# Average pooling by four over 64 x 256 x 8192: 64 KB runs per partition and a two-level pair sum in place of 32 KB runs and a reduction

## The chip, the cores and the metric

The kernel runs on one core of a Trainium2 chip. The metric is the device time of one execution in microseconds (us), as the median of several runs. Engine names: DVE is VectorE, ACT is ScalarE, SP is SyncE (here it only issues DMAs), POOL is GpSimd. TensorE is not used. 1 MB is 10^6 bytes and 1 KB is 1024 bytes here.

## What is computed

```python
x = np.random.randn(64, 256, 8192).astype(np.float32); kernel_size = stride = 4
out_len = (length - kernel_size) // stride + 1          # 2048
for i in range(out_len):
    output[:, :, i] = np.mean(x[:, :, 4*i : 4*i + 4], axis=2)
```

The windows don't overlap, and each row of 8192 gives 2048 means. The input is 536.87 MB and the output 134.22 MB, each read or written once, so 671.09 MB pass through the DMA engines whatever the tiling.

## The kernel before

The input is seen as 16384 rows of 8192 floats. `_packed_fast_path` (L215) takes 512 rows at a time with F = 4: partition p holds rows 4p to 4p+3 of the macro-tile, which lie one behind the other in DRAM, 128 KB in all. There are 32 macro-tiles.

In each of the first 31, the loop over f runs four times. L245 loads one row per partition on SP's queue: 128 partitions x 32 KB, 4096 KB in one DMA, into one of three buffers `xt` of the pool `xin`. L246 is one `tensor_reduce` on DVE that sums groups of four, 8192 values to 2048. L252 multiplies these by 1/4 on ACT, in place in `ot`. After four rows, L253 stores `ot` (32 KB per partition, 4096 KB) from ACT's queue. `ot` has two buffers.

The last macro-tile is cut finer. Row f = 0 is loaded whole, rows 1 and 2 in three pieces each (L263, reduced at L266, scaled at L272), and the last row in a ladder of six pieces of 1668, 2268, 1632, 1172, 844 and 608 columns (L284, reduced at L293). The results of rows 0 to 2 are stored in four parts of 6 KB per partition by SP (L292), which are issued behind the last load piece. The ladder's results are scaled by ACT and stored from ACT's queue (L309, L310), except the last piece, which DVE scales into `fin` (L300) and SP stores (L307).

The order of the work is set by the program order on each engine and by semaphores that the tile framework places. A load waits for the DVE instruction that read its buffer last (three tiles earlier), and for the DMA whose semaphore it uses again. A reduction waits for its load, and where it is the first into an `ot` buffer, for that buffer's store. SP issues loads in order, so a load that waits holds up what stands behind it on SP. All DMAs of SP (queue q1 in the profile) and of ACT (q10) run on the same 16 DMA engines, 8 partitions to an engine in a DMA of 128 partitions.

Of the kernel before, what the change touches and what calls it, by code (L numbers as in the profile page):

```python
# [7 lines left out]
_N_PARK = 4  # L8
_FINAL_COLS_TGT = 608
_LADDER_RATIO = 1.39  # L10
_NCHUNK_PRE = 3
_PACK_STORES = True
_PACK_F_MAX = 4


def _tail_ladder(total: int, k: int, final: int, ratio: float = _LADDER_RATIO,
                 max_chunks: int = 12) -> list:
    if total < 4 * final:
        return [total]
    rev = []  # L20
    s = 0
    w = float(final)
    while len(rev) < max_chunks - 1:
        wi = max(k, (int(round(w)) // k) * k)
        if s + wi > total - k:
            break
        rev.append(wi)
        s += wi
        w *= ratio
    sizes = [total - s] + rev[::-1]  # L30
    assert sum(sizes) == total and all(x > 0 and x % k == 0 for x in sizes)
    return sizes


def _even_chunks(total: int, k: int, n: int) -> list:
    n = max(1, min(n, total // k))
    q = (total // n) // k * k
    sizes = [q] * n
    sizes[-1] += total - q * n
    assert sum(sizes) == total and all(s > 0 and s % k == 0 for s in sizes)  # L40
    return sizes


@with_exitstack
def kernel(
    ctx: ExitStack,
    tc: tile.TileContext,
    x: bass.AP,
    kernel_size: bass.AP,
    stride: bass.AP,  # L50
    out: bass.AP,
):
    nc = tc.nc

    K = int(kernel_size)
    S = int(stride)
    assert K == S, "only stride == kernel_size supported"

    B, C, L = x.shape
    OL = (L - K) // S + 1  # L60
    assert OL * K <= L

    P = nc.NUM_PARTITIONS

    xf = x.flatten_outer_dims()
    of = out.flatten_outer_dims()
    rows = B * C

    inv_k = 1.0 / float(K)
    dt = x.dtype  # L70
    IL = OL * K

    if _PACK_STORES and IL == L:
        F = 0
        for cand in range(_PACK_F_MAX, 1, -1):
            if rows % (P * cand) == 0 and (rows // (P * cand)) >= 2:
                F = cand
                break
        if F >= 2 and L >= 64 * K and OL % 8 == 0 and OL * F * 4 <= 32768:
            _packed_fast_path(nc, tc, xf, of, rows, L, OL, K, F, inv_k, dt, P)  # L80
            return

    RPP = 1
    R = P * RPP
    NT = rows // R
    IL2 = RPP * L
    OL2 = RPP * OL
    fast = (
        IL == L
        and rows % R == 0  # L90
        and NT >= 6
        and IL2 >= 64 * K
        and OL % 2 == 0
    )

    if not fast:
        with (
            tc.tile_pool(name="xin", bufs=4) as pin,
            tc.tile_pool(name="res", bufs=4) as pout,
        ):  # L100
            r0 = 0
            while r0 < rows:
                rn = min(P, rows - r0)
                xt = pin.tile([P, IL], dt)
                ot = pout.tile([P, OL], dt)
                nc.sync.dma_start(out=xt[:rn], in_=xf[r0 : r0 + rn, :IL])
                nc.vector.tensor_reduce(
                    out=ot[:rn],
                    in_=xt[:rn].rearrange("p (m k) -> p m k", k=K),
                    axis=mybir.AxisListType.X,  # L110
                    op=mybir.AluOpType.add,
                )
                nc.scalar.mul(ot[:rn], ot[:rn], inv_k)
                nc.scalar.dma_start(out=of[r0 : r0 + rn], in_=ot[:rn])
                r0 += P
        return

    def xview(t):
        return xf[t * R : (t + 1) * R]

    def oview(t):
        return of[t * R : (t + 1) * R]

    ladder = _tail_ladder(IL2, K, _FINAL_COLS_TGT)
    chunks_pre = _even_chunks(IL2, K, _NCHUNK_PRE)
    fin_w = ladder[-1] // K

    with (
        tc.tile_pool(name="xin", bufs=4) as pin,
        tc.tile_pool(name="res", bufs=4) as pout,  # L130
        tc.tile_pool(name="rsv", bufs=1) as prsv,
        tc.tile_pool(name="fin", bufs=1) as pfin,
    ):
        rsv = prsv.tile([P, OL2], dt)
        fin = pfin.tile([P, fin_w], dt)

        for t in range(NT):
            xv = xview(t)
            ov = oview(t)
            xt = pin.tile([P, IL2], dt)  # L140
            ot = rsv if t == 0 else pout.tile([P, OL2], dt)

            if t == 0:
                nc.sync.dma_start(out=xt[:, :IL2], in_=xv[:, :IL2])
                nc.vector.tensor_reduce(
                    out=ot[:, :OL2],
                    in_=xt[:, :IL2].rearrange("p (m k) -> p m k", k=K),
                    axis=mybir.AxisListType.X,
                    op=mybir.AluOpType.add,
                )  # L150
                nc.scalar.mul(ot[:, :OL2], ot[:, :OL2], inv_k)
            elif t < NT - 3:
                nc.sync.dma_start(out=xt[:, :IL2], in_=xv[:, :IL2])
                nc.vector.tensor_reduce(
                    out=ot[:, :OL2],
                    in_=xt[:, :IL2].rearrange("p (m k) -> p m k", k=K),
                    axis=mybir.AxisListType.X,
                    op=mybir.AluOpType.add,
                )
                nc.scalar.mul(ot[:, :OL2], ot[:, :OL2], inv_k)  # L160
                nc.scalar.dma_start(out=ov[:, :OL2], in_=ot[:, :OL2])
            elif t < NT - 1:
                c0 = 0
                for cw in chunks_pre:
                    c1 = c0 + cw
                    o0, o1 = c0 // K, c1 // K
                    nc.sync.dma_start(out=xt[:, c0:c1], in_=xv[:, c0:c1])
                    nc.vector.tensor_reduce(
                        out=ot[:, o0:o1],
                        in_=xt[:, c0:c1].rearrange("p (m k) -> p m k", k=K),  # L170
                        axis=mybir.AxisListType.X,
                        op=mybir.AluOpType.add,
                    )
                    nc.scalar.mul(ot[:, o0:o1], ot[:, o0:o1], inv_k)
                    nc.scalar.dma_start(out=ov[:, o0:o1], in_=ot[:, o0:o1])
                    c0 = c1
            else:
                nchunk = len(ladder)
                c0 = 0
                for i, cw in enumerate(ladder):  # L180
                    c1 = c0 + cw
                    o0, o1 = c0 // K, c1 // K
                    last = i == nchunk - 1
                    nc.sync.dma_start(out=xt[:, c0:c1], in_=xv[:, c0:c1])
                    if last:
                        q0 = 0
                        qw = (OL2 - q0) // _N_PARK
                        for qi in range(_N_PARK):
                            qa = q0 + qi * qw
                            qb = q0 + (qi + 1) * qw if qi != _N_PARK - 1 else OL2  # L190
                            nc.sync.dma_start(
                                out=oview(0)[:, qa:qb], in_=rsv[:, qa:qb]
                            )
                    nc.vector.tensor_reduce(
                        out=ot[:, o0:o1],
                        in_=xt[:, c0:c1].rearrange("p (m k) -> p m k", k=K),
                        axis=mybir.AxisListType.X,
                        op=mybir.AluOpType.add,
                    )
                    if last:  # L200
                        nc.vector.tensor_scalar(
                            out=fin[:, :fin_w],
                            in0=ot[:, o0:o1],
                            scalar1=inv_k,
                            scalar2=None,
                            op0=mybir.AluOpType.mult,
                        )
                        nc.sync.dma_start(out=ov[:, o0:o1], in_=fin[:, :fin_w])
                    else:
                        nc.scalar.mul(ot[:, o0:o1], ot[:, o0:o1], inv_k)  # L210
                        nc.scalar.dma_start(out=ov[:, o0:o1], in_=ot[:, o0:o1])
                    c0 = c1


def _packed_fast_path(nc, tc, xf, of, rows, L, OL, K, F, inv_k, dt, P):  # L215
    R = P * F
    NTM = rows // R

# [10 lines left out]
    with (  # L229
# [6 lines left out]
        for t in range(NTM):  # L236
            xv = xe(t)
# [109 lines left out]
```

## Time and profile before

| what | value |
|---|---|
| runs (3) | median 1561.2 us, 1561.01 to 1561.22 |
| span of the profiled execution | 1559.0 us, first to last instruction |
| median less that span | 2.2 us |
| DVE busy | 1112.8 us, 71% of the span, 138 instructions |
| ACT busy | 247.4 us, 16% of the span, 137 instructions |
| HBM read, written | 536.87 MB, 134.22 MB |
| mean rate of the DMA engines | 430 GB/s over the span |

The profiled execution has no time of its own beside its span; the 2.2 us are start and end of an execution, outside the instructions, and are taken as they are. The page gives busy time per engine and, in 40 equal slices of 39 us, the busy share in tenths (9 is 90% or more). A DMA queue's share is the time that its packets took, as a share of 16 engines over the span. In rows of instructions, "idle before" is how long the engine had stood still and what ended that. A packet is one row of one DMA on one DMA engine, and each engine ends its part of a DMA with a packet of 4 bytes that counts a semaphore up.

### The profile page before, as it was taken

The page shows a single profiled execution, that of the slowest core. Times are in us where ns is not written, and L with a number is a line of the kernel's source. Part 1 is how long each engine was busy: PE and PEld are TensorE (multiplying, and loading weights), DVE is VectorE, ACT ScalarE, POOL GpSimd, SP SyncE. Part 2 cuts the span into 40 slices and gives each one's busy share as a digit, 9 for nine tenths or more (in the row PEclk, how much of TensorE's full clock was granted, in tenths as well). Part 3 has the DMA queues.
Part 4 walks back from the last instruction along what each step waited for, and adds up shares of the span by engine and source line. Part 5 has one row for each costly group of instructions (what it writes and reads, how often), then busy time and mean ns, then how long its engine had stood idle before and what let it go on. Part 6 is the DMA issues. An engine that isn't in the chain of part 4 may idle for free.

```text
span 1559.0 us, 724 instructions
## 1 busy us (share of the span) xinstructions
DVE 1112.8 (71%) x138; ACT 247.4 (16%) x137; POOL 0.2 (0%) x4
## 2 busy tenths in 40 slices
DVE  6777667776667866677666776667766677766786
ACT  1111111111111111111111111111111111111111
POOL 0000000000000000000000000000000000000000
DMA  9999999999999999999999999999999999999999
GB/s 416 418 430 436 437 432 430 430 430 432 439 433 430 430 432 430 438 434 431 430 432 430 435 434 433 431 431 430 433 437 433 432 430 431 430 437 434 432 427 384
DMA packets 25637, 671.14 MB, mean 430 GB/s; under 512 B 2848, under 2 KB 3488, under 8 KB 4768
## 3 DMA queue, kind: packets, MB, share of 16 engines
q1 hardware_dynamic: 20448, 540.10, 80.6%
q10 hardware_dynamic: 5184, 131.00, 19.5%
q14 instruction: 5, 0.04, 0.0%
HBM read 536.87 MB, written 134.22 MB: 430 GB/s over the span
## 4 chain that ended last, share of the span: by engine, by line
DMA 75%; DVE 24%; issue 0%; SPq 0%; DVEq 0%
DMA xt<-in_x_dram 75%; DVE ot L246 23%; DVE ot L293 1%; DVE ot L266 0%; SPq L263 0%; DVEq L246 0%; DVE fin L300 0%
## 5 line engine op out<-in xcount | busy, mean ns | idle before, releaser
L246 DVE TENSOR_REDUCE ot<-xt 128x2048 f32<-128x8192 f32 x124 | 1077.1, 8686 | 430.2 <-DMA xt<-in_x_dram 430.2
L252 ACT ACTIVATE ot<-ot 128x2048 f32<-128x2048 f32 x124 | 237.0, 1911 | 1270.2 <-DVE ot L246 1270.2
L266 DVE TENSOR_REDUCE ot<-xt 128x682 f32<-128x2728 f32 (+2 forms) x7 | 26.6, 3809 | 6.9 <-DMA xt<-in_x_dram 6.9
L272 ACT ACTIVATE ot<-ot 128x682 f32<-128x682 f32 (+2 forms) x7 | 6.6, 936 | 25.8 <-DVE ot L266 25.8
L293 DVE TENSOR_REDUCE ot<-xt 128x417 f32<-128x1668 f32 (+5 forms) x6 | 9.0, 1568 | 0.0
L309 ACT ACTIVATE ot<-ot 128x417 f32<-128x417 f32 (+4 forms) x5 | 2.6, 521 | 5.2 <-DVE ot L293 5.2
L252 ACT ACT_TABLE_LOAD x1 | 1.3, 1283 | 0.7 <-PEq L328 0.7
L300 DVE TENSOR_SCALAR fin<-ot 128x152 f32<-128x152 f32 x1 | 0.2, 239 | 0.0
L328 POOL MEMSET const-bfloat16-1.0<- 128x1 bf16 x1 | 0.1, 102 | 0.0
L328 POOL MEMSET const-uint8-127<- 128x1 uint8 x1 | 0.1, 102 | 0.0
L328 POOL MEMSET const-float32-0.0<- 128x1 f32 x1 | 0.1, 99 | 0.2 <-issue 0.2
L328 POOL MEMSET const-float32-1.0<- 128x1 f32 x1 | 0.1, 99 | 0.0
## 6 DMA issues: line engine op xcount, KB each, us to landing
xt<-in_x_dram SPq DMA_DIRECT2D x125, 4096.0 KB, 26.4
out_dram<-ot ACTq DMA_DIRECT2D x31, 4096.0 KB, 23.2
xt<-in_x_dram SPq DMA_DIRECT2D x4, 1364.0 KB, 23.4
out_dram<-ot SPq DMA_DIRECT2D x4, 768.0 KB, 7.7
xt<-in_x_dram SPq DMA_DIRECT2D x2, 1368.0 KB, 29.5
xt<-in_x_dram SPq DMA_DIRECT2D x1, 1134.0 KB, 16.2
xt<-in_x_dram SPq DMA_DIRECT2D x1, 834.0 KB, 22.6
xt<-in_x_dram SPq DMA_DIRECT2D x1, 816.0 KB, 17.8
```

The source lines that it names most:

```text
L246: nc.vector.tensor_reduce(out=ot[:, o0 : o0 + OL], in_=xt[:, :L].rearrange("p (m k) -> p m k", k=K), axis=mybir.AxisListType.X, op=mybir.A ...
L252: nc.scalar.mul(ot[:, o0 : o0 + OL], ot[:, o0 : o0 + OL], inv_k)
L266: nc.vector.tensor_reduce(out=ot[:, o0:o1], in_=xt[:, c0:c1].rearrange("p (m k) -> p m k", k=K), axis=mybir.AxisListType.X, op=mybir.AluOp ...
L272: nc.scalar.mul(ot[:, o0:o1], ot[:, o0:o1], inv_k)
L293: nc.vector.tensor_reduce(out=ot[:, o0:o1], in_=xt[:, c0:c1].rearrange("p (m k) -> p m k", k=K), axis=mybir.AxisListType.X, op=mybir.AluOp ...
L300: nc.vector.tensor_scalar(out=fin[:, :fin_w], in0=ot[:, o0:o1], scalar1=inv_k, scalar2=None, op0=mybir.AluOpType.mult,)
L309: nc.scalar.mul(ot[:, o0:o1], ot[:, o0:o1], inv_k)
L328: nc = _bacc.Bacc("TRN2", target_bir_lowering=False, num_devices=1)
```

## The change

The tensors are now seen as flat streams: 32 groups of 128 partitions x 32768 floats (the same 128 KB per partition as a macro-tile before). A group is loaded in two DMAs of 16384 floats per partition (64 KB in one run, 8192 KB a DMA) into two buffers `xt`, in place of four DMAs of 32 KB into three buffers. The `tensor_reduce` is replaced by two `tensor_tensor` adds on DVE: neighbours are added in pairs, 16384 values to 8192, written over the first half of `xt` (new L51), and these again in pairs, 8192 to 4096, into `ot` (new L56). ACT scales 4096 at a time in place of 2048 (new L57). The store of a group is as before, 4096 KB from ACT's queue (new L88), for groups 0 to 29.

In the last group the second load is made in two pieces, 11264 and 5120 columns (new L70). Behind them SP issues the store of the whole of group 30 (L76), that of the first half of group 31 (L77), and after each piece's scale that piece's store (L84). The ladder, the pieces of the two rows ahead of it, the store in four parts and DVE's own scale are gone; ACT issues no store in the last two groups. The paths for other shapes are removed too, and were not used by these shapes.

The buffers take 2 x 64 KB and 2 x 32 KB per partition, against 3 x 32 KB, 2 x 32 KB and a small one before.

```diff
+LOAD = 16384
+PER_STORE = 2
+LAST = (11264, 5120)
...
+    run = LOAD * PER_STORE
+    groups = total // (P * run)
...
+    pin = ctx.enter_context(tc.tile_pool(name="xin", bufs=2))
+    pout = ctx.enter_context(tc.tile_pool(name="res", bufs=2))
...
+    def pool(xt, at, width, ot, to):
+        half = width // 2
+        four = xt[:, at : at + width].rearrange("p (m k) -> p m k", k=2)
+        nc.vector.tensor_tensor(
+            out=xt[:, at : at + half], in0=four[:, :, 0], in1=four[:, :, 1], op=ADD
+        )
+        two = xt[:, at : at + half].rearrange("p (m k) -> p m k", k=2)
+        o = ot[:, to : to + width // K]
+        nc.vector.tensor_tensor(out=o, in0=two[:, :, 0], in1=two[:, :, 1], op=ADD)
+        nc.scalar.mul(o, o, inv_k)
...
+    for g in range(groups):
+        ot = pout.tile([P, run // K], dt)
+        end = g == groups - 1
+        for j in range(PER_STORE):
+            xt = pin.tile([P, LOAD], dt)
+            last = end and j == PER_STORE - 1
+            pieces = LAST if last else (LOAD,)
...
+            for w in pieces:
+                nc.sync.dma_start(
+                    out=xt[:, at : at + w], in_=xg[g][:, j * LOAD + at : j * LOAD + at + w]
+                )
...
+            if last:
+                nc.sync.dma_start(out=og[g - 1], in_=held[:, :])
+                nc.sync.dma_start(
+                    out=og[g][:, : j * LOAD // K], in_=ot[:, : j * LOAD // K]
+                )
+            for at, w in spans:
+                to = (j * LOAD + at) // K
+                pool(xt, at, w, ot, to)
+                if last:
+                    nc.sync.dma_start(
+                        out=og[g][:, to : to + w // K], in_=ot[:, to : to + w // K]
                     )
+        if g < groups - 2:
+            nc.scalar.dma_start(out=og[g], in_=ot[:, :])
+        held = ot
...
-                    nc.sync.dma_start(out=xt[:, :L], in_=xv[:, f * L : (f + 1) * L])
-                    nc.vector.tensor_reduce(
-                        out=ot[:, o0 : o0 + OL],
-                        in_=xt[:, :L].rearrange("p (m k) -> p m k", k=K),
-                        axis=mybir.AxisListType.X,
...
-                    nc.scalar.mul(ot[:, o0 : o0 + OL], ot[:, o0 : o0 + OL], inv_k)
-                nc.scalar.dma_start(out=ov[:, : F * OL], in_=ot[:, : F * OL])
...
```

More of the change, by code (lines that the diff above doesn't have):

```diff
@@ L6 @@
 from concourse._compat import with_exitstack
[L8 to L41, printed above, removed]
+ADD = mybir.AluOpType.add
+LOAD = 16384
+PER_STORE = 2
+LAST = (11264, 5120)
 @with_exitstack
@@ L55 @@
     K = int(kernel_size)
[L56 to L61, printed above, removed]
+    assert K == 4 and int(stride) == 4 and x.shape[-1] % 4 == 0
     P = nc.NUM_PARTITIONS
[L65 to L69, printed above, removed]
     dt = x.dtype
[L71 to L93, printed above, removed]
-    )
[L96 to L106, printed above, removed]
-                nc.vector.tensor_reduce(
-                    out=ot[:rn],
-                    in_=xt[:rn].rearrange("p (m k) -> p m k", k=K),
-                    axis=mybir.AxisListType.X,
-                    op=mybir.AluOpType.add,
-                )
[L113 to L149, printed above, removed]
-                )
[L151 to L172, printed above, removed]
-                    )
[L174 to L212, printed above, removed]
@@ L215, in _packed_fast_path @@
-def _packed_fast_path(nc, tc, xf, of, rows, L, OL, K, F, inv_k, dt, P):
-    R = P * F
-    NTM = rows // R
-    ladder = _tail_ladder(L, K, _FINAL_COLS_TGT)
-    chunks_pre = _even_chunks(L, K, _NCHUNK_PRE)
-    fin_w = ladder[-1] // K
-    def xe(t):
-        return xf[t * R : (t + 1) * R].rearrange("(p f) m -> p (f m)", f=F)
-    def oe(t):
-        return of[t * R : (t + 1) * R].rearrange("(p f) m -> p (f m)", f=F)
-    with (
-        tc.tile_pool(name="xin", bufs=3) as pin,
-        tc.tile_pool(name="res", bufs=2) as pout,
-        tc.tile_pool(name="fin", bufs=1) as pfin,
-    ):
-        fin = pfin.tile([P, fin_w], dt)
-        for t in range(NTM):
-            xv = xe(t)
-            ov = oe(t)
-            ot = pout.tile([P, F * OL], dt)
-            if t < NTM - 1:
-                for f in range(F):
-                    xt = pin.tile([P, L], dt)
-                    o0 = f * OL
-                    nc.sync.dma_start(out=xt[:, :L], in_=xv[:, f * L : (f + 1) * L])
-                    nc.vector.tensor_reduce(
-                        out=ot[:, o0 : o0 + OL],
-                        in_=xt[:, :L].rearrange("p (m k) -> p m k", k=K),
-                        axis=mybir.AxisListType.X,
-                        op=mybir.AluOpType.add,
-                    )
-                    nc.scalar.mul(ot[:, o0 : o0 + OL], ot[:, o0 : o0 + OL], inv_k)
-                nc.scalar.dma_start(out=ov[:, : F * OL], in_=ot[:, : F * OL])
-                continue
-            for f in range(F - 1):
-                xt = pin.tile([P, L], dt)
-                widths = [L] if f < F - 3 else chunks_pre
-                c0 = 0
-                for cw in widths:
-                    c1 = c0 + cw
-                    o0, o1 = f * OL + c0 // K, f * OL + c1 // K
-                    nc.sync.dma_start(
-                        out=xt[:, c0:c1], in_=xv[:, f * L + c0 : f * L + c1]
-                    )
-                    nc.vector.tensor_reduce(
-                        out=ot[:, o0:o1],
-                        in_=xt[:, c0:c1].rearrange("p (m k) -> p m k", k=K),
-                        axis=mybir.AxisListType.X,
-                        op=mybir.AluOpType.add,
-                    )
-                    nc.scalar.mul(ot[:, o0:o1], ot[:, o0:o1], inv_k)
-                    c0 = c1
-            fq = F - 1
-            xt = pin.tile([P, L], dt)
-            hold = fq * OL
-            nchunk = len(ladder)
-            c0 = 0
-            for i, cw in enumerate(ladder):
-                c1 = c0 + cw
-                o0, o1 = fq * OL + c0 // K, fq * OL + c1 // K
-                last = i == nchunk - 1
-                nc.sync.dma_start(
-                    out=xt[:, c0:c1], in_=xv[:, fq * L + c0 : fq * L + c1]
-                )
-                if last:
-                    qw = hold // _N_PARK
-                    for qi in range(_N_PARK):
-                        qa = qi * qw
-                        qb = (qi + 1) * qw if qi != _N_PARK - 1 else hold
-                        nc.sync.dma_start(out=ov[:, qa:qb], in_=ot[:, qa:qb])
-                nc.vector.tensor_reduce(
-                    out=ot[:, o0:o1],
-                    in_=xt[:, c0:c1].rearrange("p (m k) -> p m k", k=K),
-                    axis=mybir.AxisListType.X,
-                    op=mybir.AluOpType.add,
-                )
-                if last:
-                    nc.vector.tensor_scalar(
-                        out=fin[:, :fin_w],
-                        in0=ot[:, o0:o1],
-                        scalar1=inv_k,
-                        scalar2=None,
-                        op0=mybir.AluOpType.mult,
-                    )
-                    nc.sync.dma_start(out=ov[:, o0:o1], in_=fin[:, :fin_w])
-                else:
-                    nc.scalar.mul(ot[:, o0:o1], ot[:, o0:o1], inv_k)
-                    nc.scalar.dma_start(out=ov[:, o0:o1], in_=ot[:, o0:o1])
-                c0 = c1
@@ new lines @@
+    inv_k = 1.0 / K
+    run = LOAD * PER_STORE
+    total = x.shape[0] * x.shape[1] * x.shape[2]
+    groups = total // (P * run)
+    assert groups * P * run == total and groups >= 2
+    xg = x.flatten_outer_dims().rearrange("r l -> (r l)").rearrange("(g p w) -> g p w", p=P, w=run)
+    og = out.flatten_outer_dims().rearrange("r l -> (r l)").rearrange(
+        "(g p w) -> g p w", p=P, w=run // K
+    )
+    pin = ctx.enter_context(tc.tile_pool(name="xin", bufs=2))
+    pout = ctx.enter_context(tc.tile_pool(name="res", bufs=2))
@@ new lines @@
+    held = None
+    for g in range(groups):
[5 more added lines that the diff above has]
+            pieces = LAST if last else (LOAD,)
+            at = 0
+            spans = []
+            for w in pieces:
+                nc.sync.dma_start(
+                    out=xt[:, at : at + w], in_=xg[g][:, j * LOAD + at : j * LOAD + at + w]
+                )
+                spans.append((at, w))
+                at += w
+            if last:
+                nc.sync.dma_start(out=og[g - 1], in_=held[:, :])
+                nc.sync.dma_start(
+                    out=og[g][:, : j * LOAD // K], in_=ot[:, : j * LOAD // K]
+                )
+            for at, w in spans:
[4 more added lines that the diff above has]
+                        out=og[g][:, to : to + w // K], in_=ot[:, to : to + w // K]
+                    )
+        if g < groups - 2:
+            nc.scalar.dma_start(out=og[g], in_=ot[:, :])
+        held = ot
```

## Prediction, made before the changed kernel was run

> **What bounds the kernel now.** I read the page first, its slices and queues:
>
> ```profile
> DMA  9999999999999999999999999999999999999999
> GB/s 416 418 430 436 437 432 430 430 430 432 439 433 430 430 432 430 438 434 431 430 432 430 435 434 433 431 431 430 433 437 433 432 430 431 430 437 434 432 427 384
> ...
> q1 hardware_dynamic: 20448, 540.10, 80.6%
> q10 hardware_dynamic: 5184, 131.00, 19.5%
> ```
>
> The DMA engines are busy in every slice, and the loads' queue and the stores' queue together take 100.1% of 16 engines. That is saturation from first to last, not on average. The chain of waits gives 24% to DVE, which is misleading: a load waits for the reduction that frees its buffer, but others are still queued when it is issued. The timeline of the start shows that the work keeps step with the transfers:
>
> ```profile
> 12.74 8.69 DVE L246 TENSOR_REDUCE ot<-xt 128x2048 f32<-128x8192 f32 x1 [12.74 <-DMA xt<-in_x_dram]
> ...
> 22.43 8.69 DVE L246 TENSOR_REDUCE ot<-xt 128x2048 f32<-128x8192 f32 x1 [1.01 <-DMA xt<-in_x_dram]
> ...
> 32.14 8.69 DVE L246 TENSOR_REDUCE ot<-xt 128x2048 f32<-128x8192 f32 x1 [1.03 <-DMA xt<-in_x_dram]
> ```
>
> Each reduction starts as its load lands, 9.70 us after the one before. An engine moves 8 rows in that time, 1.213 us a row, and 4.194 MB in 9.70 us is 432 GB/s. Beside a store, loads land 14.49 us apart (149.50 to 163.99 in the timeline): 12 packets of 1.21, so loads and stores alternate and none is lost. Stage by stage, the busy times by window say where the rate falls:
>
> ```profile
> 100.00:1500.00 1400.00, 1000.30 (x116) 221.61 (x116) 0.00 (x0) 1.00 1.00 433
> 1500.00:1540.00 40.00, 33.12 (x8) 7.69 (x7) 0.00 (x0) 1.00 1.00 425
> 1540.00:1550.00 10.00, 9.91 (x8) 3.38 (x6) 0.00 (x0) 1.00 1.02 413
> 1550.00:1555.00 5.00, 0.00 (x0) 0.00 (x0) 0.00 (x0) 1.00 1.03 407
> 1555.00:1559.00 4.00, 0.00 (x0) 0.00 (x0) 0.00 (x0) 1.00 0.25 96
> ```
>
> Columns: window, length, busy DVE, ACT, POOL, clock, DMA share, GB/s. The middle runs at 433. Only the last 20 us, with their small pieces, are slower. So the bytes don't change, the end is set by the DMA queues, and there is little to win: packets, the tail, and nothing from DVE. 671.09 MB at 433 GB/s are 1549.9 us of the 1559.0.
>
> **The change, part by part.**
>
> *Fewer packets.* The trace's packet records (one entry per packet, no view prints them) give these medians:
>
> ```
> bytes   4   608  2432  6144  10912  32768
> ns      9    31    98   234    411   1213
> ```
>
> The slope from 608 to 32768 is (1213-31)/32160 = 0.03675 ns a byte, which leaves 8.7 ns a packet. But the next packet opens before the last one closes: starts on one engine lie 1209.5 ns apart, and 1209.5 less 32768 x 0.03675 is about 5 ns. I take 5, since the distance of starts is what a saturated engine pays. Its ends are 0 (a run of 64 KB is still moved as two packets, or the fee goes by bytes) and 8.7. A loss I exclude: the records are linear over a factor of 54 in size. Now an engine has (20448+5184)/16 = 1602 packets, 178 of them semaphores (one a DMA), 1424 of data. After: 65 loads and 34 stores of 8 rows, 792 of data and 99 semaphores. The 63 full loads merge 504; 128 more go with the small pieces.
> - merging: 504 x 5 = 2.5 us (0 to 504 x 8.7 = 4.4)
> - small pieces: 128 x 5 = 0.6 us (to 1.1)
> - semaphores: 79 x 6 ns between starts = 0.5 us (to 0.7)
>
> Together 3.6 us, from 1.1 to 6.2.
>
> *The tail.* Before, reads and writes of 0.6 to 9 KB a row mix. Against 433 GB/s the windows lack 10 x 20/433 = 0.5 us, 5 x 26/433 = 0.3, and in the last 4 us, of which the DMAs ran 3.1 (to 1558.1), 3.1 less 4 x 96/433 = 2.2: 3.0 us. After, behind the last load stand 4.2 MB of group 30 and 2.1 MB of group 31, 14.6 us at 433, on one queue and pure writes. Under them lies the work on the last pieces. Piece one lands 6.0 us ahead of piece two; DVE needs about 9.1 us for it and 4.2 for piece two, ACT 1.3 more. The last store is thus issued some 9 us after the last landing, and 11 with the issue delay below: covered by 14.6 us. If that cover were gone, the excess would stand at the end in full. Some scatter of the engines stays; I take 2.0 of the 3.0 back, ends 0 and 3.0.
>
> *DVE.* TENSOR_TENSOR is not in this trace. The reductions give 8686 ns for 8192 inputs and 778 for 608: 1.043 ns a step and 144 ns fixed. The only elementwise row, L300's TENSOR_SCALAR, takes 239 ns for 152, (239-144)/152 = 0.63 a step, so a step of an elementwise instruction is no dearer than a reduction's. An add that takes a pair each step: 8192 x 1.043 + 144 = 8.69 us, and 4096 give 4.42, 13.1 a tile, against two reductions' 17.4. If every value read is a step (2 a pair), it is 17.2 + 8.7 = 25.9. I take 13.1 by the nearest row, and neither end gains anything: what decides is when the next load is issued. Least issue to landing is 12.0 us (the view of the input tile), less 9.70 of moving: 2.3 us. A load is ready 13.1 + 2.3 = 15.4 us after its buffer's tile landed, while the other buffer's load lasts 2 x 9.68 = 19.4. Slack is 4.0 us, against 2 x 9.70 - 8.7 - 2.3 = 8.4 now with three buffers. Beside a store the load lasts 29 us and the slack is 13.6. So the smaller DVE time costs and wins nothing, and the lost buffer costs nothing.
>
> [...]
>
> *Waits on queues.* SP's load waits now on DVE's second add; behind it on SP stands only the next load, and at the end the parked stores, which would be behind the loads on the DMA rings anyway. A store takes 29 us in place of 23.2, as 8 rows of 1.21 alternate with 8 of 2.42. Who waits for it is new L56 two groups on: at 3 x 24.2 + 8.7 = 81 us after the group's second tile landed, when the store ends at 13.1 + 3.7 (ACT, 1911 ns doubled) + 2 + 29 = 48. Nothing. ACT's time falls off the path as now.
>
> [...]
>
> *Start.* First packets are issued as before, and DVE's first work at 22 us in place of 12.7 delays nothing but the third load (issued at 35, ready at 37, the second lands at 41). Zero.
>
> **Sum.** 1559.0 - 3.6 - 2.0 = 1553.4 us of span, and with the 2.2 around it 1555.6. Ends: -1.1 and -9.2, so 1560.1 and 1552.0.
>
> **Rivals.**
> 1. *The runs aren't merged* (64 KB is moved as two packets, or a packet's fee goes by bytes). For it: no record here is over 32 KB. Against: the instruction carries one run of 64 KB a row. Then 1.1 + 2.0 = 3.1: 1558.1; 1560.1 if the tail gives nothing either.
> 2. *DVE becomes the bound, slower.* One mechanism: the adds read two values from SBUF at each step, 8 bytes apart, in the same partition, and take two steps. With only two buffers the DMA engines run dry as soon as DVE's tile passes 19.4 - 2.3 = 17.1 us (beyond that every us over costs up to 64). At 25.9 it is 22 + 64 x 25.9 + 10 of tail = 1690 of span, 1692. For it: the operation has no row, and the slack halves. Against: the 0.63 ns above.
> 3. *The tail gives nothing back* but packets do: 1557.6, told within the forecast's range.
>
> **How the numbers follow.** A change within 0.2% (3.1 us) can't be told from none. Forecast, 1555.6 with 1552.0 to 1558.6 about it (rival 3 in it): 0.66, of which 0.62 is faster by over 0.2%. Rival 1: 0.22, half below 1558.1 and half within 0.2%: 0.11 and 0.11. Rival 2: 0.12, slower. So faster 0.73, same 0.15, slower 0.12. The range is 1552.0 to 1561.0, the ends of the unknown costs and 0.9 for scatter; it leaves out rival 2 and little else.
>
> **What would show it.** Packets: the queues' counts fall to about (520+32+69) x 16 = 9936 on q1 and 30 x 9 x 16 = 4320 on q10; q1 near 18000 means rival 1. Middle: 433 to 434 GB/s at DMA share 1.00, adds of 8.7 and 4.4 us, and loads landing 19.4 and 29 us apart in turn. A share under 0.98 in the middle, or adds of 17 us, means rival 2. Tail: over 420 GB/s until 3 us before the end. I am wrong if the span changes by more than 7 us with the middle at 433, since then the time is in something that I haven't named.

## The result, and the profile after

The changed kernel takes 1576.05 us (1569.3 to 1581.1, four runs) against 1561.11 (1560.88 to 1561.22): ratio 1.0093, interval 1.0065 to 1.0122, slower by 0.9%. The forecast was 1555.6 and the range ended at 1561.0. Note the scatter too: 12 us between runs, where the kernel before has 0.3.

The page after (slices of 39.5 us, queues, DVE's groups):

```profile
span 1579.3 us, 492 instructions
...
DMA  9999999999999999999999999999999999999998
GB/s 425 416 432 427 437 424 425 427 435 430 428 428 419 442 425 423 419 431 427 427 425 425 432 422 428 422 428 416 431 432 418 427 420 427 443 415 420 416 435 369
...
q1 hardware_dynamic: 9936, 545.26, 81.3%
q10 hardware_dynamic: 4320, 125.83, 18.5%
...
L51 DVE TENSOR_TENSOR xt<-xt 128x8192 f32<-128x8192 f32 (+1 forms) x65 | 556.5, 8561 | 722.0 <-DMA xt<-in_x_dram 721.9
...
L56 DVE TENSOR_TENSOR ot<-xt 128x4096 f32<-128x4096 f32 (+1 forms) x65 | 283.4, 4360 | 3.9
```

The packet counts are those forecast, so 64 KB are one packet each. DVE is idle for 722 us, waiting for loads. The DMA engines are as busy as before, yet they move 425 GB/s in place of 430. By window, the middle has it (length, DVE, ACT, POOL, clock, DMA share, GB/s):

```profile
100.00:1500.00 1400.00, 749.93 (x116) 206.12 (x57) 0.00 (x0) 1.00 1.00 427
```

A share of 1.00 at 427, where it was 1.00 at 433. The engines never lack work; some packets take longer. The packet records say which:

```
load packets            size    median ns   mean ns   over the median by 32 ns or more
before                  32768        1213      1217      51 of 16000
after                   65536        2418      2468     800 of  8064
```

The excess over the median, summed over all load packets and divided by 16 engines, is 25.0 us after and 3.8 before. And it lies in one place: 24 of the 25 us belong to packets that start between 4 us before and 14 us after ACT issues a store. The timeline around one store shows it at work (adds on a landed tile, and the issue of a store):

```profile
1075.69 8.69 DVE L51 TENSOR_TENSOR xt<-xt 128x8192 f32<-128x8192 f32 x1 [16.87 <-DMA xt<-in_x_dram]
...
1092.52 0.34 ACTq L88 DMA_DIRECT2D out_dram<-ot  x1
1095.02 8.69 DVE L51 TENSOR_TENSOR xt<-xt 128x8192 f32<-128x8192 f32 x1 [6.18 <-DMA xt<-in_x_dram]
...
1124.92 8.69 DVE L51 TENSOR_TENSOR xt<-xt 128x8192 f32<-128x8192 f32 x1 [16.69 <-DMA xt<-in_x_dram]
```

Two loads land 19.33 and 29.90 us apart, 49.23 for a group of 16.8 MB read and 4.2 written; the kernel before takes 48.47 (from one store's issue at 101.88 to the next at 150.35). The load without a store, 19.33, is as forecast. The store is issued 2.5 us ahead of a landing. What follows on two of the engines is this (start in us, L a load packet, S a store packet, duration in ns where it isn't 2418 or 1213; the records don't name the engine, so each chain is put together by time, a packet where the one before it ends):

```
1093.20 L          1095.61 L (3702)   1099.31 S   1100.52 L          1102.93 S
1093.46 L (2831)   1096.29 S          1097.50 L (3513)   1101.01 S   1102.22 L
```

The load packets around the store's first packet last up to 1.3 us longer, and this on every engine. A packet or two later all is normal. So 30 stores at some 0.8 us are the loss, and it is more than the gain. (49.23 - 48.47) x 30 = 23 us, less some 2.5 us that the rest of the run gained, is the span's change of 20.3.

### The profile page after: what moved, and what is told of

Its sections match the earlier page's. It is cut to its first block, busy times and chain, and to the rows that moved or that the text cites. A ratio compares the mean times of both kernels' runs of the same rounds, so it can differ in the third digit from the quotient of the medians.

```text
span 1579.3 us, 492 instructions
## 1 busy us (share of the span) xinstructions
DVE 839.8 (53%) x130; ACT 232.9 (15%) x66; POOL 0.2 (0%) x4
## 3 DMA queue, kind: packets, MB, share of 16 engines
q1 hardware_dynamic: 9936, 545.26, 81.3%
q10 hardware_dynamic: 4320, 125.83, 18.5%
## 4 chain that ended last, share of the span: by engine, by line
DMA 72%; DVE 27%; issue 0%; ACT 0%; SPq 0%
DMA xt<-in_x_dram 72%; DVE xt L51 18%; DVE ot L56 9%; ACT ot L57 0%; SPq L70 0%
## 5 line engine op out<-in xcount | busy, mean ns | idle before, releaser
L51 DVE TENSOR_TENSOR xt<-xt 128x8192 f32<-128x8192 f32 (+1 forms) x65 | 556.5, 8561 | 722.0 <-DMA xt<-in_x_dram 721.9
L57 ACT ACTIVATE ot<-ot 128x4096 f32<-128x4096 f32 (+1 forms) x65 | 231.6, 3564 | 1333.3 <-DVE ot L56 1333.3
L56 DVE TENSOR_TENSOR ot<-xt 128x4096 f32<-128x4096 f32 (+1 forms) x65 | 283.4, 4360 | 3.9
```

Of the source, the lines that this page charges most:

```text
L51: nc.vector.tensor_tensor(out=xt[:, at : at + half], in0=four[:, :, 0], in1=four[:, :, 1], op=ADD)
L56: nc.vector.tensor_tensor(out=o, in0=two[:, :, 0], in1=two[:, :, 1], op=ADD)
L57: nc.scalar.mul(o, o, inv_k)
```

## The experiments

**First set.** My first theory, S, was that the packet's size does it: 64 KB packets are stretched at every start of a store. Its rival P was the place at which the store starts.

*e1_half_rows*: each 64 KB load in two DMAs of 32 KB rows (`HALF` is 8192).

```diff
-                nc.sync.dma_start(
-                    out=xt[:, at : at + w], in_=xg[g][:, j * LOAD + at : j * LOAD + at + w]
-                )
+                for c in range(at, at + w, HALF):
+                    cw = min(HALF, at + w - c)
+                    nc.sync.dma_start(
+                        out=xt[:, c : c + cw], in_=xg[g][:, j * LOAD + c : j * LOAD + c + cw]
+                    )
```

> Every 64 KB load of the changed kernel is made as two DMAs of 32 KB rows into the two halves of the same buffer; adds, scales, stores and their order stay. Theory S (a load packet of 64 KB is stretched when a store starts on the other queue, 0.8 us per engine and store, 25 us in all): the stretching goes with the packet size, the stores start 48.5 us apart in place of 49.2, 1556 to 1560 us. Theory P (the place: the store now starts just where one load gives way to the next, with two buffers only): packets of 32 KB are stretched as well, 1570 to 1580 us.

Measured 1569.88 us, ratio 1.0057 (1.0042 to 1.0072). The time lies a hair under P's range. Packets of 32 KB are stretched as well, 567 of 16384, 13.0 us per engine. S falls; half of the cost may still go with the size.

*e6_store_halves*: each store in two, one behind each tile's scale.

```diff
                 pool(xt, at, w, ot, to)
+                if g < groups - 2:
+                    nc.scalar.dma_start(
+                        out=og[g][:, to : to + w // K], in_=ot[:, to : to + w // K]
+                    )
...
-        if g < groups - 2:
-            nc.scalar.dma_start(out=og[g], in_=ot[:, :])
```

> The changed kernel with every store of a group made in two halves, one behind each tile's scale (2048 KB, 16 KB rows): 60 starts of a store in place of 30 for the same bytes. Theory S with its cost per start: another 20 to 27 us, 1592 to 1608 us. If the cost goes with the bytes stored beside loads, or with how unlike the packets are, it stays within 5 us of 1576 or grows by the 2 us of more packets.

Measured 1555.55 us, ratio 0.9965 (0.9952 to 0.9978), faster than either of the two ranges that I had (1592 to 1608 by S, within 5 us of 1576 otherwise). Its timeline:

```profile
1076.83 0.34 ACTq L84 DMA_DIRECT2D out_dram<-ot  x1
1084.17 8.69 DVE L51 TENSOR_TENSOR xt<-xt 128x8192 f32<-128x8192 f32 x1 [11.02 <-DMA xt<-in_x_dram]
1101.06 0.34 ACTq L84 DMA_DIRECT2D out_dram<-ot  x1
1108.36 8.69 DVE L51 TENSOR_TENSOR xt<-xt 128x8192 f32<-128x8192 f32 x1 [10.98 <-DMA xt<-in_x_dram]
```

A tile lands every 24.2 us, which is 8 x (2.418 + 0.611) with the 611 ns that a 16 KB packet takes at the end of the changed kernel, and the stores follow each other without a pause (issued 24.13 to 24.24 us apart from the fourth to the 56th): store packets alternate with load packets all the time, and the step from loads alone to both happens once. Its load packets have a mean of 2421 ns. That 64 KB packets beside stores are no harm is shown here. What saves this run isn't shown: its stores never pause, but each is also issued 7.3 us ahead of a landing, and no run here separates the two.

*e2_sp_stores*: SP issues each store behind the load two tiles ahead, so that there is one queue.

```diff
+        if n + 2 < ntiles:
+            load(n + 2)
+        if j == PER_STORE - 1 and not last:
+            nc.sync.dma_start(out=og[g], in_=ot[:, :])
```

> The 64 KB loads stay, but each group's store is issued by SP, behind the load made two tiles ahead, so that all DMAs stand in one queue in order and no two queues are served in turn. Theory S and theory P both need two queues at once: no stretching, median 64 KB packet and mean both 2418 ns, 1552 to 1557 us. If a 64 KB read simply suffers from writes being made at the same time by other engines, or from two buffers only, it stays at 1566 to 1580 us.

Measured 1558.01 us, ratio 0.9981 (0.9972 to 0.9991), a little over what was expected. 4.6 us of stretch per engine remain, most of it in the first 500 us. Without two queues served in turn the cost is nearly gone.

*e3_before_pairs*: the kernel before with pair adds in place of `tensor_reduce`.

> The kernel before with only the sums changed: two levels of pair adds in place of each reduction. Both theories: the adds lie under the transfers, 4.43 + 2.29 = 6.7 us a row in place of 8.69, and the time stays within 1 us of 1561.1. If the adds themselves slow the transfers (they read SBUF at twice the rate), it is 1566 us or more.

Measured 1561.78 us, ratio 1.0004 (0.9994 to 1.0013): the sums cost and win nothing, as forecast.

**Second set: the place.** ACT multiplies the group's second half by 1.0 some more times before it issues the store; the output doesn't change, only the store's moment. The number in `range` is 2 in f1, 1 in f3, 4 in g1, 6 in g2 and 8 in i1.

```diff
         if g < groups - 2:
+            for _ in range(2):
+                nc.scalar.mul(ot[:, LOAD // K :], ot[:, LOAD // K :], 1.0)
             nc.scalar.dma_start(out=og[g], in_=ot[:, :])
```

> The changed kernel, with two more ACT multiplications by 1.0 (3.62 us each, on the second half of the group's result) between a group's last scale and its store: the store is issued 24 us after its tile landed instead of 16.8, so 4.7 us behind the change from one load to the next instead of 2.5 us ahead of it. Theory P (what costs is a store that starts as the load queue goes from one DMA to the next): the load packets aren't stretched, 1553 to 1560 us. Rival Q (what costs is that loads alone give way to loads and stores in turn with one load queued instead of two, wherever that happens): 1568 to 1580 us as before.

Measured 1554.69 us, ratio 0.9959 (0.9944 to 0.9974): faster than both kernels, and all that it adds to the changed one is 7.3 us of useless work on ACT before each store. Its middle and one group:

```profile
100.00:1500.00 1400.00, 757.16 (x116) 419.50 (x116) 0.00 (x0) 1.00 1.00 434
```

```profile
1078.11 8.69 DVE L51 TENSOR_TENSOR xt<-xt 128x8192 f32<-128x8192 f32 x1 [8.61 <-DMA xt<-in_x_dram]
1080.48 0.34 ACTq L90 DMA_DIRECT2D out_dram<-ot  x1
...
1126.46 8.69 DVE L51 TENSOR_TENSOR xt<-xt 128x8192 f32<-128x8192 f32 x1 [8.63 <-DMA xt<-in_x_dram]
1128.81 0.34 ACTq L90 DMA_DIRECT2D out_dram<-ot  x1
```

The store is issued 2.4 us behind a landing (4.7 was expected) in place of 2.5 ahead, and a group takes 48.33 us in place of 49.23. The stretch is 2.2 us per engine in the whole run, half of it at the first store.

> The same with one multiplication: the store is issued 20.4 us after its tile landed, 1.1 us behind the change of loads, about where the kernel before has it (0.9 us). Theory P: 1553 to 1562 us. Rival Q: 1568 to 1580 us.

Measured 1570.53 us, ratio 1.0059 (1.0042 to 1.0076): P had 1562 at most, and the time lies in Q's range, 1568 to 1580. A delay that puts the issue on the landing itself (within 0.35 us, stores 3 to 30) doesn't help; "as before, 0.9 us behind" was not reached, since the stores drifted. P alone was too coarse.

The same in the kernel before, three multiplications of the last row's 2048 results ahead of each store:

> The kernel before with three more ACT multiplications by 1.0 (1.91 us each) ahead of each 4096 KB store, which is then issued 16.6 us after its last row landed, 2.8 us ahead of a change of loads instead of 0.9 us behind one. Theory P: load packets are stretched now in the kernel before as well, 0.4 to 0.9 us per store, 1568 to 1590 us. Rival Q (two loads still queued): 1561 us, unchanged within 1 us.

Measured 1565.65, 1569.26 and 1571.24 us, ratio 1.0049 (1.0032 to 1.0066); a fourth run took 1590.9 and is left out. The kernel before, with its 32 KB rows, reductions and three buffers, loses 8 us by the store's place alone, a little over half of what the changed one lost. Q is refuted by this and by f1.

> The kernel before with macro-tiles of two rows per partition in place of four: 62 stores of 2048 KB (16 KB rows) in place of 31 of 4096 KB, the same place of issue behind a load's landing. By packets alone 256 more per engine at 5 ns and 31 more semaphores: plus 1.5 us, 1562 to 1563. If the number of starts cost 0.8 us each even here: 1580 us or more. If stores spread more evenly are a gain of their own with 32 KB packets too: under 1560.5.

The edit is `_PACK_F_MAX = 2`. Measured 1561.87 us, ratio 1.0005 (0.9996 to 1.0015): 62 starts cost only their packets. They weren't where I expected them: the store is issued 2.0 us after DVE is done, as before, but the landings moved, and it lies 0.2 to 1.2 us ahead of one (stores 3 to 62, the median 0.25) and not 0.9 behind. Its stretch is 0.01 us per engine and store. With 32 KB rows, then, a store just ahead of a landing is free.

**Third set: how far the good place reaches, and what the merging is worth.**

> The changed kernel with four multiplications by 1.0 (14.5 us) ahead of each store: it is issued 31.3 us after its tile landed, 12 us behind one change of loads and 7.4 ahead of the next. Theory P (a store that starts near the change from one load to the next costs 0.4 to 0.9 us, elsewhere nothing): 1553 to 1556 us, as with two. Rival L (later is better: what costs is a store soon after a load's issue, 3.7 us before and 11 us in the good run): the next load is issued 1.2 us after the store, and the time is 1565 us or more, or in between.

Measured 1554.73 us, ratio 0.996 (0.9946 to 0.9974). The store settles 7.3 us behind a landing, where I had expected 12. P.

> With six (21.7 us): the store is issued 38.5 us after its tile landed, 0.2 us ahead of the next change of loads, as early relative to it as the run with one. Theory P: the cost comes back, 1565 to 1580 us. Rival D (any delay over 7 us is enough, because the store then no longer meets the scales and adds of its own group): 1553 to 1556 us.

Measured 1555.42 us, ratio 0.9964 (0.9951 to 0.9977), in rival D's range. But it did not test what it was meant to: since a late store lies beside other loads, their landings move too, and its stores were issued 12 us behind one and 9.6 ahead of the next. It is one more good place; i1 below speaks against D.

> The loads in halves of 32 KB rows, with two multiplications ahead of the store: the place that cost nothing with 64 KB rows, and the packets of the kernel before. Theory P: no stretching; against the run with 64 KB rows in the same place it shows what the merged packets are worth by themselves, by 5 ns a packet and 63 more semaphores 2.9 us, so 1557 to 1558.5 us. If 32 KB packets don't differ from 64 KB ones: 1554.7 us. If the place is only good with 64 KB packets: 1563 us or more.

Measured 1560.55 us, ratio 0.9999 (0.999 to 1.0009). No stretch beyond that of the kernel before (3.9 us). The time is above P's range, since the rows are worth more: against f1 5.9 us, twice what was expected.

**Fourth set: measured against what?** In every bad run the store had also been issued 3.3 to 7.8 us after SP's last load issue (theory I), not only near the change of loads (theory W).

> The kernel before with two ACT multiplications by 1.0 (1.91 us each) ahead of each 4096 KB store: issued 5.8 us after SP's last load issue, and 4.8 us behind the change from one load to the next, 4.9 ahead of the following one. Theory W (cost only near that change): 1560 to 1562 us. Theory I (cost 3.6 to 7.9 us after a load's issue): 1566 us or more, as with three multiplications.

Measured 1561.53 us, ratio 1.0003 (0.9994 to 1.0013): W.

> The kernel before with pair adds and one multiplication by 1.0 ahead of the store: issued 3.8 us after SP's last load issue, and 0.8 us behind the change of loads, as in the kernel before (0.9). Theory W: 1561 to 1562.5 us, as with pair adds alone. Theory I: 1566 us or more.

Measured 1561.71 us, ratio 1.0004 (0.9994 to 1.0014): W.

```diff
         nc.scalar.mul(o, o, inv_k)
+        if width == LOAD:
+            nc.vector.tensor_scalar(
+                out=xt[:, at : at + 3584], in0=xt[:, at : at + 3584], scalar1=1.0,
+                scalar2=None, op0=mybir.AluOpType.mult,
+            )
```

> The changed kernel with one more DVE instruction behind the two adds of each tile (a multiplication by 1.0 of 3584 columns of the spent input buffer, about 2 us), which only makes the next load wait: its issue moves from 3.7 to about 1.6 us ahead of the store's, while the store keeps its place of 2.5 us ahead of the change of loads. Theory W: 1568 to 1580 us as before. Theory I: 1553 to 1558 us.

Measured 1574.62 us, ratio 1.0095 (1.0064 to 1.0127): W, and I is refuted three times.

> The changed kernel with eight multiplications by 1.0 (29 us) ahead of each store: issued 45.7 us after its tile landed. The previous store then lies beside the first of the two loads that follow, so that the changes of loads come 29 and 48.4 us after the landing, and the store is issued 2.7 us ahead of the second, as far ahead of a change as in the changed kernel. Theory W: the cost is back, 1565 to 1580 us. Rival (any late place is good): 1554.5 to 1556 us.

Measured 1562.49 us (1557.86 to 1569.88), ratio 1.0007 (0.9992 to 1.0021). The stores settled 0.7 us behind a landing in the median (0.3 ahead to 0.9 behind), not 2.7 ahead. The time lies between the two ranges, and part of the cost is back: 13.1 us of stretch per engine in the profiled execution, and the scatter between runs as well. A late place alone isn't a good one.

**All stores together.** From the traces (f2 left out, whose profiled execution was far above its median, and e2, where SP stores): the median place of a run's stores from the third on, against the nearest landing of a load, that is, the moment at which the slowest of the 16 engines reports its part. The stretch is the excess of the load packets that start from 4 us before the issue to 14 us after it. (DVE starts 0.02 to 0.1 us after the landing, so these places differ a little from those read off DVE above.)

```
store issued                      load rows   mean stretch per engine and store
7.3 us behind                     64 KB       0.01 us   g1
4.8 and 4.9 behind                32 KB       0.03      g3, h1
2.4 behind                        64 KB       0.01      f1
1.0 behind                        32 KB       0.03      before, h3
0.7 behind (0.3 ahead to 0.9)     64 KB       0.32      i1
on it (0.35 ahead to 0.3 behind)  64 KB       0.45      f3
0.2 to 1.2 ahead                  32 KB       0.01      f4
1.0 ahead                         32 KB       0.03      e3
2.5 ahead                         64 KB       0.81      changed kernel; h2 0.88
2.5 ahead                         32 KB       0.38      e1
7.3 ahead                         64 KB       0.00      e6
9.6 ahead                         64 KB       0.01      g2
```

With 64 KB rows a store costs 0.3 to 0.9 us on each engine when it is issued 2.5 us ahead of a landing or within 0.9 us of one, and nothing from 2.4 us behind or 7 ahead; what lies between was not tried. With 32 KB rows it costs 0.38 us at 2.5 ahead and nothing in the other places tried, just ahead of a landing among them (e3, f4). So the place decides, but no one window holds for both sizes, and the distance from a landing isn't the whole rule: in i1 stores 6 to 14, 0.6 to 0.9 us behind, cost 0.01 to 0.09 us, and later ones 0.76 to 0.85 behind cost 0.27 to 0.60.

Why the packets are stretched there stays open. The engines get out of step in most bad runs: from the first of the 16 to the last, a load lands within 1.3 us in the median in the kernel before, and within 4.0 in the changed one. But being apart isn't enough, since in e6 it is 2.4 us throughout, at no cost; and h2, with the dearest stores, has 2.5. The first store of nearly every run costs 0.75 to 1.1 us wherever it lies, in the kernel before too (0.97); in e6 it costs 0.15. No run here looks inside an engine.

## Why the prediction was wrong

The step that failed is "Waits on queues" together with "Beside a store, loads land 14.49 us apart ... so loads and stores alternate and none is lost". I read the steady alternation of the kernel before and took its cost of nothing for a property of stores beside loads. It was a property of the place in time: there, ACT issues the store 0.9 us behind a landing, and its first packets follow 3.4 to 4.7 us later on the 16 engines (medians of the first and the last), 4.3 to 5.5 us into a load of 9.7. The change moved that place without a line of the diff saying so. DVE's 13.1 us and ACT's 3.6 put the issue 16.8 us after the landing, 2.5 ahead of the next at 19.4. I had worked out each of these numbers (13.1, 3.7, 19.4), but only against buffers and slack. Price: 30 x 0.8 = 24 us of stretch. That the place does it is shown by f1 and g1 (the same rows, sums and buffers, the store later, the loss gone), by h2 (the place kept, the loss kept) and by f2 (the kernel before, moved, loses too); what happens inside an engine there is not.

Point by point:
- *DVE*: right. 8692 and 4425 ns for the full tiles against 8.69 and 4.42. Rival 2 fell, e3 shows that DVE is off the path (773 us of work in the middle 1400 in place of 1000, at ratio 1.0004), and the loss of a buffer did not starve the engines (share 1.00).
- *Packets*: counts right to the last (9936 and 4320), and 2418 ns a packet against 1213 + 32768 x 0.03675 = 2417. The term was too small: I chose 5 ns a packet by the spacing in a stage of loads alone. A group takes 48.37 us in f1 against 48.53 before (means over stores 3 to 30), 0.17 x 32 = 5.4 us, where merging and its share of semaphores had 2.9. The upper end, 8.7 ns a packet, was nearer. In loads alone the fee is as small as I took it (19.35 for 64 KB against 2 x 9.70).
- *Tail*: too large. In f1, which ends as the changed kernel does, the last 19 us lack 10 x 13/434 + 5 x 15/434 + (3.2 - 4 x 152/434) = 2.3 us where the kernel before lacked 3.0 (3.2 and 3.1 us run to the last store's landing). So 0.7 came back, not 2.0. In the changed kernel itself nothing did, by the same working for its last 19 us (422, 402 and 63 GB/s against 433): 0.3 + 0.4 + 2.8 = 3.4 us. The view of f1:

```profile
1534.00:1544.00 10.00, 6.10 (x3) 3.82 (x2) 0.00 (x0) 1.00 0.98 421
1544.00:1549.00 5.00, 0.00 (x0) 0.00 (x0) 0.00 (x0) 1.00 0.98 419
1549.00:1553.00 4.00, 0.00 (x0) 0.00 (x0) 0.00 (x0) 1.00 0.37 152
```

- *The sum*: 1555.6 is what the change is worth where its store is well placed (f1 1554.69, e6 1555.55). That the number fits so well is partly luck, because two sizes were off in opposite directions. The forecast lacked one term, with the other sign.
- *The rivals*: none named it. The slower one looked for an engine that starves, to be seen as a share under 0.98. The loss came with the share at 1.00. The last sentence of the prediction does not apply either, since the middle fell from 433 to 427.

## What to carry to other kernels

When two DMA queues are served in turn and the kernel is bound by them, work out when each store is issued against the end of the load in flight, before and after a change; here, with 64 KB rows, a store issued 2.5 us ahead of that end or within 0.9 us of it cost 0.3 to 0.9 us each, and 7 us of delay, or stores in halves (e6, no extra work for DVE or ACT, 1555.55 us), took it away. The window isn't a rule to carry over: with 32 KB rows a part of it was free, so try two or three delays. A busy share of 1.00 is no proof of full rate (427 GB/s in the changed kernel, 433 before, both at 1.00): compare the rate of the stage, and the mean with the median duration of equal packets (2468 and 2418 ns). And a wide scatter between runs of a kernel (12 us here, against 0.3) can be a sign of it: the changed kernel, h2 and i1 spread over some 12 us, f1 and g1 over less than 1; but e1 and f3, which lose too, over less than 2.

## What the runs showed of the hardware

- A row of 64 KB moved as one packet of 2418 ns, and in a good place that was worth 5.4 us of 1559 over rows of 32 KB (by groups; 5.9 between f1 and g3).
- Loads and stores alternated packet by packet. In the changed kernel (rows of 64 KB read, 32 written) a load of eight rows per engine lands 29.4 to 30.4 us after the one before it beside a store, 8 x (2.418 + 1.213) = 29.05 and the stretch; in e6 (64 and 16 KB) 24.2 us, 8 x (2.418 + 0.611). In the kernel before (32 and 32 KB) two loads in four land 14.5 us after the one before (13.3 to 15.7), the others 9.7 to 9.8.
- Load packets were stretched from 2418 to as much as 4067 ns in the changed kernel, while the engines count as busy throughout (share 1.00 from 100 to 1500 us).
- A first store cost 0.97 us per engine in the kernel before, where the later ones cost 0.03 each, and 0.75 to 1.1 in nearly every run; in e6 it cost 0.15.
